# Embedding pieces moved later in the w_out stage, their results kept in the ring of raw pieces, embedding loads and gatings moved, and the last five output blocks started on preset PSUM banks

## The chip, the cores and the metric

The kernel runs on one core of a Trainium2 chip. The metric is device time of one execution in microseconds (us). Several executions are timed; another one is taken by the hardware profiler. Data is float32 throughout. "Piece" below is a block of weights of 128 x 1024 float32 (512 KB): two k-slices of 128 x 512.

## What is computed

One layer: a sliding-window attention mixer, then a per-layer embedding that is added through a gate, then a last norm (512 rows of x, D = 2048).

```python
def reference(x, p, norm_g, final_g, rel_bias, swa_w_in, swa_w_out, ..., ple_proj, ple_norm, ple_gate):
    for i in range(DEPTH):                       # DEPTH = 1, mixer 0
        hn = rmsnorm(x, norm_g[i])
        y = swa_mixer(hn, swa_w_in[j], swa_w_out[j], swa_sinks[j], rel_bias)
...
        x = x + y
        emb = p[i] @ ple_proj[i]                 # 512 x 256 @ 256 x 2048
        g = jax.nn.sigmoid(rmsnorm(x, ple_norm[i]) @ ple_gate[i])
        x = x + emb * g
    return rmsnorm(x, final_g)

def swa_mixer(h, w_in, w_out, sinks, rel_bias):
    q, k, v, gate = jnp.split(h @ w_in, ...)
...
    return (out * jax.nn.silu(gate)) @ w_out
```

## The kernel before

**Precision.** Every product of two float32 matrices is made of three matmuls: each operand is split into a high part (float32r) and the remainder. `mm3` issues the three (lines 126 to 128). For each piece of weights, ScalarE (ACT) casts the raw piece to its high part (`bhi`, line 755) and VectorE (DVE) subtracts for the low part (`blo`, line 756).

**Stages.** First the projections to q, k, v and gate with the attention, then the w_out product, then the ple_gate product, then the last norm and the stores. The w_out and the ple_gate product use a scheme of block products in the manner of Strassen: the products p go in the order 1, 7, 6, 5, 3, 4, each in two column halves jj, each half in four pieces m. "Piece (6,1,2)" is p = 6, jj = 1, m = 2. One piece is 12 matmuls of 512 columns. A further quadrant of each product is computed by the same scheme one level deeper, its "small" products threaded between the pieces (`SMALL`; `small_steps` and `ple_steps` say behind which piece their operands are prepared).

**Embedding.** p @ ple_proj needs nothing of x, so it is threaded into the w_out stage. Nine extra pieces of ple_proj (slots k = 0 to 8), each of 12 matmuls too, stand behind the pieces of w_out that `EMBED_AT` lists. Their accumulators (`eX`, `eO`, `eY`, `eW`, `eZ`) are PSUM banks of 512 columns which are opened by ACT: a slot may begin with a bank that holds minus another one (lines 1253 and 1275), and its matmuls add to it. A finished quadrant (c, jj) is copied by ACT or DVE out of PSUM into an SBUF tile, and GpSimd (POOL) stores it to DRAM (`embeds`, line 1236, 512 KB). Before, there are two such SBUF tiles, `to[0]` and `to[1]`, the two halves of the buffer s2 (in the profile `s`); `to[1]` holds p itself at first. `embed_steps` says behind which pieces p is loaded, split (`make_forms`, DVE lines 1209 to 1221), and the pieces of ple_proj are loaded and summed (`sums0`, `sums1`, DVE lines 1173 and 1174). In the ple_gate stage SP loads the quadrants again into two buffers `e` (`load_embeds`, line 1366, at the places in `embed_loads`), and `gated` applies sigmoid (ACT, line 1379), multiplies by e (DVE, line 1381), adds to x (line 1385, or a POOL DMA that accumulates) and sums squares (line 1396).

**Order.** Each engine runs its instructions in the order of the program. PE and SP have the order of the code throughout; DVE, ACT and POOL have it from the second block product of the ple_gate stage on, before that a scheduler orders them. Raw pieces are requested by SP a fixed number of pieces ahead (`ahead`, line 774: 6 in the "far" range from w_out piece (6,0,0) to the start of the ple_gate stage, 4 after it), and split two pieces ahead of their use. In the far range they lie in a ring of eight buffers of 4 KB a partition, tag `grown`. In the ple_gate stage this ring holds the eight pieces of the last product p = 4.

**End.** The last product p = 4 has weights that are split early (`split_last`, lines 763 and 764, behind the pieces that `early` lists; before: six in p = 3, two behind it). It is computed as blocks (jj, tb) of 24 matmuls: (0,0), (1,0), (0,1), and (1,1) in two parts of 288 and 224 columns. Three of them go to a fresh bank, and DVE subtracts s2 from the result (line 1553); the two parts of (1,1) go to banks that ACT has opened with minus s2 (line 1535). After a block, gate, x and squares follow; finished rows are scaled by 1/norm and final_g (`row`, DVE, line 1414; `by_gain`, DVE, line 1406) and stored.

Of the kernel before, what the change touches and what calls it, by code (L numbers as in the profile page):

```python
# [11 lines left out]
F32 = mybir.dt.float32  # L12
# [6 lines left out]
D = 2048  # L19
# [36 lines left out]
def trunk_kernel(ctx: ExitStack, tc: tile.TileContext, a: dict):  # L56
# [602 lines left out]
    def blk(t):  # L659
# [60 lines left out]
    class Pieces:  # L720
# [48 lines left out]
        def ahead(self, i):  # L769

            last = len(self.specs) - 9
            for n in range(max(i, 0), min(i + 6, last) + 1):
                kind = self.specs[n][0]
                if n not in self.base and n >= self.done and kind not in ("grow", "emb") and (kind == "seed" or n <= i + (6 if far_from <= n < far_to else 4 if i >= far_to else 3)):
# [20 lines left out]
    def add_stage(nm, order):  # L795
# [26 lines left out]
    EMBEDS = {  # L822
        (6, 1): [(1, 0)], (5, 0): [(1, 1), (5, 0)], (5, 1): [(5, 1)], (3, 0): [(3, 0)], (3, 1): [(3, 1)],
    }
# [232 lines left out]
    class Small:  # L1057
# [67 lines left out]
    small_steps = {  # L1125
        (5, 0, 2): 1, (5, 1, 0): 7, (5, 1, 2): 7, (5, 1, 3): 6, (3, 0, 1): 6, (3, 0, 2): 2, (3, 1, 0): 5, (3, 1, 2): 5,
        (3, 1, 3): 4, (4, 0, 1): 3, (4, 0, 3): 3,
    }
# [5 lines left out]
    class Embedding:  # L1134


        def __init__(self, at):
            self.at, self.done = at, 0
            flat = lambda v: v.rearrange("p a b c -> p (a b c)")
            v1, v7 = flat(s1), flat(s7)  # L1140
            self.b1, self.b4, self.b5 = v7[:, :512], v7[:, 512:WE], v7[:, WE:]
            self.b2, self.b3 = v1[:, :WE], v1[:, WE:]
            self.to = [s2[:, n] for n in range(2)]
            self.forms, self.X, self.temp = {}, {}, {}
            self.next = 0
# [7 lines left out]
        def prepare(self, step):  # L1153
# [7 lines left out]
            if step == "p":  # L1161
                load(self.to[1], a["pT"])
            elif step == "forms":
# [28 lines left out]
        def make_forms(self):  # L1192
            r = self.to[1]
            high, low = (late.tile([P, WE], F32R, tag="e", name=f"p_{v}", bufs=2) for v in ("high", "low"))
# [37 lines left out]

        def keep(self, c, jj, n, fill):
            for tb in range(2):
                fill(self.to[n][:, tb], tb)
            nc.gpsimd.dma_start(embeds[c, jj], self.to[n])

        def slot(self):

            k = self.done  # L1240
            jj = 0 if k < 5 else 1
            piece = B.get(self.at[k])
            if k == 0:
                self.left()
            if k in (4, 8):
                self.times(4, piece, 0, self.Z)
                self.keep(4, jj if k == 8 else 0, 1, lambda to, tb: nc.scalar.copy(to, self.Z[tb]))
            if k in (0, 4):
                self.X = self.bank_pair("eX", "t")
                self.times(1, piece, 1 if k else 0, self.X, True)  # L1250
                self.O = self.bank_pair("eO", "o")
                for tb in range(2):
                    nc.scalar.mul(self.O[tb], self.X[tb], -1.0)
            elif k in (1, 5):
                self.times(2, piece, 0, self.O)
                self.times(6, piece, 1, self.X)
                self.keep(1, jj, 0, lambda to, tb: nc.scalar.copy(to, self.O[tb]))
                self.Y = self.bank_pair("eY", "o")
                for tb in range(2):
                    nc.scalar.copy(self.Y[tb], self.X[tb])  # L1260
            elif k in (2, 6):
                self.times(7, piece, 0, self.Y)
                self.times(3, piece, 1, self.X)
                for tb in range(2):
                    nc.scalar.copy(self.left_of[:, tb], self.Y[tb])
                for tb in range(2):
                    nc.scalar.copy(self.to[0][:, tb], self.X[tb])
            elif k in (3, 7):
                self.W = self.bank_pair("eW", "o")
                self.times(5, piece, 0, self.W, True)  # L1270
                self.keep(5, jj, 1, lambda to, tb: nc.vector.tensor_add(to, self.W[tb], self.left_of[:, tb]))
                self.keep(3, jj, 0, lambda to, tb: nc.vector.tensor_add(to, self.W[tb], to))
# [91 lines left out]
    def load_embeds(c, jj):  # L1364
        t = embed_of[c, jj] = late.tile([P, 2, 512], F32, tag="e", name=f"e{c}_{jj}", bufs=2)
        nc.sync.dma_start(t, embeds[c, jj])

    embed_loads = {
        (6, 1, 0): (1, 0), (6, 1, 2): (1, 1), (5, 0, 3): (5, 0), (5, 1, 3): (5, 1), (3, 0, 1): (3, 0), (3, 1, 1): (3, 1),
        (3, 1, 3): (4, 0),  # L1370
# [79 lines left out]
    rooms4 = {}  # L1450
    early = {(3, 0, 0): 0, (3, 0, 2): 1, (3, 1, 0): 2, (3, 1, 1): 3, (3, 1, 2): 4, (3, 1, 3): 5}

# [18 lines left out]
    for n, p in enumerate(ORDER_PLE[:-1]):  # L1471
# [8 lines left out]
        for jj in range(2):  # L1480
            calls = iter(range(4))

            def todo():
# [16 lines left out]
                if k is not None:  # L1500
                    split_last(k)

            def between(m, ps):
# [5 lines left out]
                for q in SMALL["ple_gate"].get((p, jj), {}).get(m, ()):  # L1509
                    small_ple.product(q)  # L1510

            ps = unit(p, jj, at_ple, ple_forms, todo, between)
# [3 lines left out]
            for of, which in EMBEDS.get((p, jj), ()):  # L1516
                e = {t: embed_of[of, which][:, t % 2] for t in ((2, 3) if of == 5 else (0, 1))}
                held_e.update(e)
                if of == 1:
                    later.insert(which ^ 1, partial_of(gate_later, "sum", which, None, dict(e)))  # L1520
                    held_e.clear()
# [9 lines left out]

    def opened_bank(jj, tb, tag, c):

        ps = bank(f"open{jj}_{tb}_{c.start}", tag)
        nc.scalar.mul(ps[:, c], s2[:, jj, tb, c], -1.0)
        return ps

    def block(jj, tb, tag, c=slice(0, 512), share=1.0, opened_ps=None):

        ps = bank(f"last{jj}_{tb}_{c.start}", tag) if opened_ps is None else opened_ps  # L1540
        for k in range(8):
# [3 lines left out]
                ps[:, c], fh[:, k % 2, blk(tb)], fl[:, k % 2, blk(tb)], bh[k % 2][:, c], bl[k % 2][:, c],  # L1545
                k == 0 and opened_ps is None, k == 7, opened_ps is not None,
            )
        e, z = embed_of[4, jj][:, tb], s2[:, jj, tb, c]

        def opened():  # L1550
            if opened_ps is not None:
                return gated(2 + tb, jj, ps[:, c], z, e, c, share)
            nc.vector.tensor_sub(z, ps[:, c], z)
            return gated(2 + tb, jj, z, z, e, c, share)

        return opened

# [6 lines left out]
    load_embeds(4, 1)  # L1564
    split_last(6)
    split_last(7)
    for g in two:
        run(g)
# [5 lines left out]
    next(root)  # L1574
    g = block(0, 0, "s")()
    run(root)
    for step in moved.pop():
        step()
    next(g)
    for j in range(4):  # L1580
        row(0, j, yn2[:, 0:1])
        store(0, j)
    next(g)
    run(g)
    lower, upper = slice(0, 288), slice(288, 512)
    lower_ps = opened_bank(1, 1, "p", lower)
    for j in range(4):
        row(1, j, yn2[:, 1:2])
        store(1, j)
    g = block(1, 0, "s")()  # L1590
    next(g)
# [8 lines left out]
    next(root)  # L1600
    g = block(0, 1, "p")()
    run(root)
    next(g)
    upper_ps = opened_bank(1, 1, "s", upper)
    for j in range(2):
# [8 lines left out]
    base, yn = (const.tile([P, 1], F32, name=f"{v}_3") for v in ("base", "yn"))  # L1614
    g = block(1, 1, "p", lower, opened_ps=lower_ps)()
    next(g)
# [3 lines left out]
    n = done[3]  # L1620
    last = block(1, 1, "s", upper, 1.0 / D, upper_ps)()
    next(last)
# [79 lines left out]
```

## Time and profile before

| | |
|---|---|
| time, median of 3 runs | 807.44 us (807.13, 807.44, 810.07) |
| profiled execution, its own time | 812.43 us |
| its span, first to last instruction | 810.7 us |
| mean granted TensorE clock | 0.986 of full |
| instructions | 11171 |
| ACT busy | 521.4 us |
| DMA, moved | 205.94 MB, mean 254 GB/s |

The durations quoted below come from the profiled execution. A row of the timeline has the start and the duration in us, the engine, the line, the operation, output and inputs by the program's names, shapes, a count of merged instructions, and in brackets how long the engine stood idle before it and what ended this. Matmuls are pipelined: one of 512 columns is listed with 0.39 us at full clock, but the next one starts 0.227 us after it. A row of a window has its bounds, its length, and for each engine the busy us with the count of instructions, then the granted clock, the share of the DMA engines and GB/s.

### The profile page before, as it was taken

How to read it: one execution, taken by the hardware profiler on the slowest of the kernel's cores; microseconds unless marked ns; L12 is line 12 of the kernel's file. 1: busy time of each engine (PE TensorE's matmuls, PEld its weight loads, DVE VectorE, ACT ScalarE, POOL GpSimd, SP SyncE). 2: the span in 40 equal slices, each digit the busy share in tenths (PEclk: the TensorE clock that was granted, in tenths of full speed). 3: DMA queues.
4: the chain of work that ended last, by engine and by line, in shares of the span. 5: the costliest groups of instructions: out<-in, count | busy, mean ns of one | idle time of the engine just before them, and what ended most of it. 6: DMA issues, size and time to landing. Idle time of an engine off the chain costs nothing. (4 is left out here: it accounts for less than half of the span.)

```text
span 810.7 us, 11171 instructions
## 1 busy us (share of the span) xinstructions
PE 786.5 (97%) x3708; PEld 654.8 (81%) x3708; DVE 615.6 (76%) x1057; ACT 521.4 (64%) x1096; POOL 146.8 (18%) x270
## 2 busy tenths in 40 slices
PE   9999999999999999999999998979999999998993
PEld 8888888888888888888888887868888888886783
DVE  4547697868877697768787998747987769978796
ACT  5742676656766576666666555657668966646853
POOL 0201323231323132231311100010000002202100
PEclk9999999999999999999999999989999999999997
DMA  8988999999999999999986698676884499997934
GB/s 332 289 205 285 218 271 299 281 306 248 283 267 282 240 268 275 270 286 249 304 217 176 232 344 293 208 269 207 263 295 173 147 341 272 267 271 196 271 125 135
DMA packets 49961, 205.94 MB, mean 254 GB/s; under 512 B 7456, under 2 KB 8480, under 8 KB 44144
## 3 DMA queue, kind: packets, MB, share of 16 engines
q1 hardware_dynamic: 39152, 154.58, 54.5%
q0 software_dynamic: 10752, 50.66, 30.9%
q8 instruction: 29, 0.48, 0.2%
q14 instruction: 28, 0.23, 0.1%
HBM read 192.31 MB, written 75.55 MB: 330 GB/s over the span
## 5 line engine op out<-in xcount | busy, mean ns | idle before, releaser
L756 DVE TENSOR_TENSOR blo<-braw,bhi 128x1024 fp32r<-128x1024 f32 x100 | 121.4, 1220 | 42.4 <-ACT bhi L755 41.8
L755 ACT CAST bhi<-braw 128x1024 fp32r<-128x1024 f32 x100 | 104.4, 1050 | 41.8 <-PE o L128 16.3
L126 PE MATMUL gps<-xh,whi 128*128 128x512 f32 x256 | 100.0, 390 | 0.0
L127 PE MATMUL gps<-xl,whi 128*128 128x512 f32 x256 | 99.9, 390 | 0.0
L128 PE MATMUL gps<-xh,wlo 128*128 128x512 f32 x256 | 99.7, 390 | 0.0
L126 PE MATMUL qps<-xh,whi 128*128 128x512 f32 x224 | 87.8, 392 | 0.0
L127 PE MATMUL qps<-xl,whi 128*128 128x512 f32 x224 | 87.4, 390 | 0.0
L128 PE MATMUL qps<-xh,wlo 128*128 128x512 f32 x224 | 87.3, 390 | 0.0
L570 POOL TENSOR_SCALAR_AFFINE_SELECT own<-r 64x512 fp32r<-64x512 f32 (+1 forms) x48 | 32.4, 675 | 243.4 <-DVE r L560 243.4
L126 PE MATMUL o<-bhi,fho 128*128 128x512 f32 x192 | 74.9, 390 | 1.4 <-ACT bhi L755 1.4
L127 PE MATMUL o<-blo,fho 128*128 128x512 f32 x192 | 75.1, 391 | 1.2 <-DVE blo L756 1.2
L110 DVE TENSOR_TENSOR wlo<-wraw,whi 128x1024 fp32r<-128x1024 f32 x60 | 73.5, 1226 | 3.0 <-ACT whi L109 2.9
L128 PE MATMUL o<-bhi,flo 128*128 128x512 f32 x192 | 74.8, 389 | 0.0
L556 ACT CAST r<-pt 128x256 fp32r<-128x256 f32 x64 | 23.9, 374 | 69.0 <-PE pt L551 68.8
L126 PE MATMUL g<-bhi,fhg 128*128 128x512 f32 x160 | 63.3, 396 | 2.5 <-DVE s L1430 2.5
L109 ACT CAST whi<-wraw 128x1024 fp32r<-128x1024 f32 x60 | 62.3, 1040 | 4.8 <-issue 4.1
L127 PE MATMUL g<-blo,fhg 128*128 128x512 f32 x160 | 63.5, 397 | 1.7 <-DVE blo L756 1.6
L128 PE MATMUL g<-bhi,flg 128*128 128x512 f32 x160 | 63.1, 394 | 0.0
L128 PEld LDWEIGHTS gps<-xh,wlo 128*128 128x128 f32 x256 | 48.1, 188 | 10.3
L126 PEld LDWEIGHTS gps<-xh,whi 128*128 128x128 f32 x256 | 48.1, 188 | 9.2
L529 ACT ACTIVATE t<-t,sm 128x129 f32<-128x129 f32 (+1 forms) x128 | 49.6, 389 | 8.7 <-DVE sm L525 7.3
L127 PEld LDWEIGHTS gps<-xl,whi 128*128 128x128 f32 x256 | 48.1, 188 | 8.8
(296 smaller groups left out, 1820.4 us busy)
## 6 DMA issues: line engine op xcount, KB each, us to landing
wraw<-in_w_gate_in SPq DMA_DIRECT2D x32, 512.0 KB, 7.9
w_out<-in_w_out POOLq DMA_DIRECT2D x32, 512.0 KB, 9.2
braw<-w_out SPq DMA_DIRECT2D x32, 512.0 KB, 6.0
wraw<-in_w_q SPq DMA_DIRECT2D x28, 512.0 KB, 6.8
braw<-in_w_out SPq DMA_DIRECT2D x22, 512.0 KB, 4.6
braw<-in_ple_gate SPq DMA_DIRECT2D x22, 512.0 KB, 8.1
xw<-in_first SPq DMA_DIRECT2D x14, 640.5 KB, 7.0
w_out<-in_w_out SPq DMA_DIRECT2D x16, 512.0 KB, 11.3
```

Source lines behind the costliest of these rows:

```text
L109: nc.scalar.copy(hi, raw)
L110: nc.vector.tensor_sub(lo, raw, hi.bitcast(F32))
L126: nc.tensor.matmul(ps, sh, mh, start=first, stop=False, skip_group_check=more)
L127: nc.tensor.matmul(ps, sh, ml, start=False, stop=False, skip_group_check=more)
L128: nc.tensor.matmul(ps, sl, mh, start=False, stop=last, skip_group_check=more)
L529: nc.scalar.activation(su, su, AF.Exp, bias=sm[:, u : u + 1], accum_out=sm[:, 2 + u : 3 + u])
L556: nc.scalar.copy(rh, src)
L570: nc.gpsimd.affine_select(out=flat(own), in_=flat(r).bitcast(F32), pattern=[[0, 8], [sign, HB]], compare_op=ALU.is_ge, fill=0.0, base=-HB ...
L755: nc.scalar.copy(hi[:, :n], raw)
L756: nc.vector.tensor_sub(lo[:, :n], raw, hi[:, :n].bitcast(F32))
```

## The change

It has five parts.

1. *Embedding later.* All nine slots stand later, the first behind piece (6,1,0) instead of (6,0,1), the last behind (3,0,0) instead of (5,1,1); the loading of p and the preparation of its operands follow. The small products of the w_out stage start later too and end closer together.
2. *Stores through the ring.* A finished quadrant is kept in a tile of its own out of the ring of eight (`made`) instead of `to[0]` and `to[1]`. p stays in s2. In return raw pieces in the far range are requested 5 ahead instead of 6.
3. *Loads and gatings.* In the ple_gate stage the embeds of three of the quadrants are loaded one to three pieces earlier, and the gating of the quadrants that need no further product (`"sum"`) is queued earlier.
4. *Opened banks.* All last five blocks go to banks that ACT has opened with minus s2 while p = 3 still runs; the three subtractions of line 1553 are gone, and the sigmoid reads PSUM. Seven pieces of the last product are split in p = 3 instead of six.
5. *Rows.* In the end phase of rows 0 to 255, DVE scales column groups 2 and 3, and ACT groups 0 and 1, whose gain DVE has multiplied in during p = 3 (`gains`).

```diff
     SMALL = {
         "w_out": {
-            (5, 1): {2: [1], 3: [1]}, (3, 0): {0: [7], 1: [7], 3: [6]}, (3, 1): {0: [6], 1: [2], 3: [2]},
-            (4, 0): {0: [5], 1: [5], 2: [4], 3: [4]}, (4, 1): {0: [3], 1: [3]},
+            (3, 0): {1: [1], 2: [1], 3: [7]}, (3, 1): {0: [7], 1: [6], 2: [6], 3: [2]},
+            (4, 0): {0: [2], 1: [5], 2: [5], 3: [4]}, (4, 1): {0: [4, 3], 1: [3]},
...
-                if n not in self.base ... n <= i + (6 if far_from <= n < far_to else 4 if i >= far_to else 3)):
+                if n not in self.base ... n <= i + (5 if far_from <= n < far_to else 4 if i >= far_to else 3)):
...
     EMBED_AT = [
-        (6, 0, 1), (6, 0, 2), (6, 1, 0), (6, 1, 1), (6, 1, 3), (5, 0, 0), (5, 0, 2), (5, 0, 3), (5, 1, 1),
+        (6, 1, 0), (6, 1, 1), (6, 1, 3), (5, 0, 0), (5, 0, 2), (5, 0, 3), (5, 1, 1), (5, 1, 2), (3, 0, 0),
...
+        def room(self, c):
+            return late.tile([P, 2, 512], F32, tag="grown", name=f"made{c}_{self.done}", bufs=8)
+
-        def keep(self, c, jj, n, fill):
+        def keep(self, c, jj, fill, to=None):
+            to = self.room(c) if to is None else to
             for tb in range(2):
-                fill(self.to[n][:, tb], tb)
-            nc.gpsimd.dma_start(embeds[c, jj], self.to[n])
+                fill(to[:, tb], tb)
+            nc.gpsimd.dma_start(embeds[c, jj], to)
...
     embed_steps = {
-        (1, 1, 2): "p", (7, 0, 1): "forms", (7, 0, 3): "load0", (7, 1, 1): "sums0", (6, 0, 2): "load1", (6, 0, 3): "load2",
-        (6, 1, 0): "load3", (6, 1, 2): "sums1",
+        (7, 1, 2): "p", (6, 0, 0): "load0", (6, 0, 1): "forms", (6, 0, 2): "sums0", (6, 1, 1): "load1", (6, 1, 2): "load2",
+        (5, 0, 0): "load3", (5, 0, 1): "sums1",
...
     embed_loads = {
-        (6, 1, 0): (1, 0), (6, 1, 2): (1, 1), (5, 0, 3): (5, 0), (5, 1, 3): (5, 1), (3, 0, 1): (3, 0), (3, 1, 1): (3, 1),
+        (6, 0, 3): (1, 0), (6, 1, 1): (1, 1), (5, 0, 1): (5, 0), (5, 1, 1): (5, 1), (3, 0, 1): (3, 0), (3, 1, 1): (3, 1),
...
+    def rows_out(t):
+        for j in (2, 3):
+            row(t, j, yn2[:, t : t + 1])
+            store(t, j)
+        for j in range(2):
+            nc.scalar.mul(x1[j][:, t, :], x1[j][:, t, :], yn2[:, t : t + 1])
+            store(t, j)
...
+    opens = {
+        (3, 1, 0): (0, 0, "t"), (3, 1, 1): (1, 0, "t"), (3, 1, 2): (0, 1, "o"), (3, 1, 3): (1, 1, "o", lower),
+    }
+    gains = {(3, 0, 1): (0, 0), (3, 0, 2): (1, 0), (3, 1, 0): (0, 1), (3, 1, 2): (1, 1)}
...
-            nc.vector.tensor_sub(z, ps[:, c], z)
-            return gated(2 + tb, jj, z, z, e, c, share)
...
+        return gated(2 + tb, jj, ps[:, c], s2[:, jj, tb, c], embed_of[4, jj][:, tb], c, share)
```

On ACT, around slot k = 4 of the embedding (line 1247 before is line 1251 now; `eZ`, `eX`, `eO` are the slot's banks, `s_5037` is s2). Before:

```order
L755 CAST bhi_5659<-braw_5569 128x1024 [waits DMAHW2_49,PE_49,Activation_49]
L865 CAST fho_10_5878<-gate_2333 128x512 [waits PE_49]
L755 CAST bhi_5677<-s_5036 128x1024 [waits DMAHW0_49,PE_49,Activation_49]
L1247 COPY s_5037<-eZ_0_5632 128x512 [waits DMASW2_49,PE_49]
L1247 COPY s_5037<-eZ_1_5633 128x512 [waits PE_49]
L1253 ACTIVATE eO_0_5698<-eX_0_5690 128x512 [waits PE_49,Activation_49]
L1253 ACTIVATE eO_1_5699<-eX_1_5691 128x512 [waits PE_49,Activation_49]
```

and of the change:

```order
L1251 COPY made_4_5753<-eZ_0_5689 128x512 [waits PE_49]
L755 CAST bhi_5743<-s_5036 128x1024 [waits DMAHW2_49,DVE_49,Activation_49]
L1251 COPY made_4_5753<-eZ_1_5690 128x512 [waits PE_49]
L1257 ACTIVATE eO_0_5765<-eX_0_5757 128x512 [waits PE_49,Activation_49]
L1257 ACTIVATE eO_1_5766<-eX_1_5758 128x512 [waits PE_49,Activation_49]
```

The copy waited for a POOL DMA (DMASW, a store of `embeds`) and for PE; now it waits for PE alone.

On SP, in the ple_gate stage around the load of the embeds of quadrant (5,0), tile `e_0`. Before:

```order
L747 DMA braw_7398<-ple_gate_1_2_832 128x1024 [waits DMAHW4_49,DMASW0_49,DVE_49]
L747 DMA braw_7422<-ple_gate_1_3_833 128x1024 [waits DMAHW5_49,DMASW1_49,DVE_49]
L1366 DMA e_0_7445<-embeds_0_5041 128x1024 [waits DMASW2_49,DVE_49]
L747 DMA braw_7448<-in_ple_gate 128x1024 [waits DMAHW6_49,DMAHW3_49,Activation_49]
L747 DMA braw_7471<-in_ple_gate 128x1024 [waits DMAHW7_49,Activation_49]
```

and of the change:

```order
L747 DMA braw_7389<-ple_gate_1_1_831 128x1024 [waits DMAHW3_49,DVE_49]
L1371 DMA e_0_7408<-embeds_0_5041 128x1024
L747 DMA braw_7414<-ple_gate_1_2_832 128x1024 [waits DMAHW4_49,DMAHW1_49,DVE_49]
L747 DMA braw_7438<-ple_gate_1_3_833 128x1024 [waits DMAHW5_49,DVE_49]
L747 DMA braw_7462<-in_ple_gate 128x1024 [waits DMAHW6_49,DVE_49]
```

The load stands two raw pieces earlier and no longer waits for DVE, that is for the gating that reads the buffer's former contents; those who read it are awaited by an earlier instruction of the queue.

On ACT at the end. `open_1_0` and `open_1_288` are the banks of the two parts of block (1,1); `s_5037` is s2. Before:

```order
L1379 ACTIVATE s_5037<-s_5037,rstd_6595 128x512 [waits DVE_49]
L1396 ACTIVATE s_5037,ssq_5035<-x1s 128x512 [waits DVE_49]
L1379 ACTIVATE s_5037<-s_5037,rstd_6595 128x512 [waits DVE_49]
L1535 ACTIVATE open_1_288_7877<-s_5037 128x224
L1609 ACTIVATE x1s<-x1s,yn_7755 128x512 [waits Pool_49]
L1609 ACTIVATE x1s<-x1s,yn_7755 128x512
```

and of the change, where line 1476 opens a bank and line 1387 is the sigmoid:

```order
L763 CAST last_7756<-grown_6975 128x1024 [waits DMASW4_49]
L1476 ACTIVATE open_1_288_7773<-s_5037 128x224 [waits Activation_49]
L1404 ACTIVATE s_5036,ssq_5035<-x1s 128x512 [waits DVE_49] x2
L1404 ACTIVATE s_5038,ssq_5035<-x1s 128x512 [waits DMASW7_49]
L1404 ACTIVATE s_5038,ssq_5035<-x1s 128x512 [waits DMASW0_49]
L1387 ACTIVATE s_5037<-open_0_0_7689,rstd_6603 128x512 [waits PE_49]
```

The opening of the last bank stood behind two sigmoids that wait for DVE; now it stands ahead of all sigmoids of the last blocks.

More of the change, by code (lines that the diff above doesn't have):

```diff
@@ L1142, in __init__ @@
             self.b2, self.b3 = v1[:, :WE], v1[:, WE:]
-            self.to = [s2[:, n] for n in range(2)]
+            self.p = s2[:, 0]
             self.forms, self.X, self.temp = {}, {}, {}
@@ L1161, in prepare @@
             if step == "p":
-                load(self.to[1], a["pT"])
+                load(self.p, a["pT"])
             elif step == "forms":
@@ L1265, in slot @@
                     nc.scalar.copy(self.left_of[:, tb], self.Y[tb])
+                self.upper = self.room(3)
                 for tb in range(2):
-                    nc.scalar.copy(self.to[0][:, tb], self.X[tb])
+                    nc.scalar.copy(self.upper[:, tb], self.X[tb])
             elif k in (3, 7):
@@ L1450, in trunk_kernel, with open_bank @@
     rooms4 = {}
-    early = {(3, 0, 0): 0, (3, 0, 2): 1, (3, 1, 0): 2, (3, 1, 1): 3, (3, 1, 2): 4, (3, 1, 3): 5}
+    early = {(3, 0, 0): 0, (3, 0, 2): 1, (3, 0, 3): 2, (3, 1, 0): 3, (3, 1, 1): 4, (3, 1, 2): 5, (3, 1, 3): 6}
+    lower, upper = slice(0, 288), slice(288, 512)
+    opened = {}
+    def open_bank(jj, tb, tag, c=slice(0, 512)):
+        ps = opened[jj, tb, c.start] = bank(f"open{jj}_{tb}_{c.start}", tag)
+        nc.scalar.mul(ps[:, c], s2[:, jj, tb, c], -1.0)
+    opens = {
+        (3, 1, 0): (0, 0, "t"), (3, 1, 1): (1, 0, "t"), (3, 1, 2): (0, 1, "o"), (3, 1, 3): (1, 1, "o", lower),
+    }
+    gains = {(3, 0, 1): (0, 0), (3, 0, 2): (1, 0), (3, 1, 0): (0, 1), (3, 1, 2): (1, 1)}
     def split_last(k):
@@ L1501, in todo @@
                     split_last(k)
+                if (p, jj, step) in opens:
+                    open_bank(*opens[p, jj, step])
+                if (p, jj, step) in gains:
+                    by_gain(*gains[p, jj, step])
             def between(m, ps):
@@ L1530, in trunk_kernel, with block @@
     f = ple_forms.made[4]
[L1532 to L1540, printed above, removed]
+    def block(jj, tb, c=slice(0, 512), share=1.0):
+        ps = opened[jj, tb, c.start]
         for k in range(8):
@@ L1574, in trunk_kernel @@
     next(root)
-    g = block(0, 0, "s")()
+    g = block(0, 0)
     run(root)
@@ L1579, in trunk_kernel @@
     next(g)
-    for j in range(4):
-        row(0, j, yn2[:, 0:1])
-        store(0, j)
+    rows_out(0)
     next(g)
     run(g)
[L1585 to L1590, printed above, removed]
+    rows_out(1)
+    g = block(1, 0)
     next(g)
@@ L1620, in trunk_kernel @@
     n = done[3]
-    last = block(1, 1, "s", upper, 1.0 / D, upper_ps)()
+    last = block(1, 1, upper, 1.0 / D)
     next(last)
```

40 lines of the change are left out of this document (19 added, 21 removed).

## The prediction

> **What bounds the kernel now.** I read the busy shares first, then the list of waits by engine, then the timeline around each wait, and windows of 10 us where a wait was spread out.
>
> ```profile
> PE 786.5 (97%) x3708; PEld 654.8 (81%) x3708; DVE 615.6 (76%) x1057; ACT 521.4 (64%) x1096; POOL 146.8 (18%) x270
> ...
> PE eO L126 <- ACT eO L1253: 4.1, 1, 4.1
> PE open L126 <- ACT open L1535: 4.0, 1, 4.0
> PE g L126 <- DVE s L1430: 2.5, 1, 2.5
> PE g L127 <- DVE blo L756: 1.6, 3, 0.8
> PE o L126 <- ACT bhi L755: 1.4, 1, 1.4
> PE o L127 <- DVE blo L756: 1.2, 3, 0.8
> ```
>
> PE is busy for 97%, and the changed program issues the same matmuls in the same number. So the change can win only what PE loses in waits, in matmuls at a lowered clock behind them, and at the end. The waits (us in total, times, longest) name four places; A, B, C and D are their names below.
>
> **A, slot k = 4 of the embedding.**
>
> ```profile
> 527.21 1.41 POOL L1236 DMA_DIRECT2D embeds<-s  x2
> 533.40 0.39 PE L128 MATMUL o<-bhi,flo 128*128 128x512 f32 x1
> 536.23 1.07 ACT L1247 COPY s<-eZ 128x512 f32<-128x512 f32 x2 [6.49 <-DMA embeds<-s]
> 537.19 1.09 ACT L1253 ACTIVATE eO<-eX 128x512 f32<-128x512 f32 x2
> 537.85 0.80 PE L126 MATMUL eO<-bhi,p_high 128*128 128x512 f32 x1 [4.06 <-ACT eO L1253]
> 542.95 0.39 PE L126 MATMUL o<-bhi,fho 128*128 128x512 f32 x1
> ...
> DMA to landing us min/median/max: 2.9/7.0/12.6
> embeds<-s POOLq DMA_DIRECT2D x8, 512.0 KB, 5.7
> ```
>
> ACT wants to copy eZ into s2, but the store that POOL issued at 527.21 still reads it: 6.49 us of idle ACT. The opening of eO stands behind the copy, and PE stands 4.06 us. Behind the wait the slot's 12 matmuls take 542.95 - 537.85 = 5.10 instead of 12 x 0.227 = 2.72 (0.227 = 9.77 us over 43 matmuls in a window below), so 2.38 more. Now the copy fills a tile of its own, and its only wait is for PE. Gain 4.06 + 2.38 = **6.4**; nothing, if ACT is late there for another reason (second rival).
>
> **B, DVE's backlog before the embedding.**
>
> ```profile
> 480.00:490.00 10.00, 9.77 (x43) 7.77 (x43) 10.00 (x15) 4.20 (x5) 0.00 (x0) 1.00 0.97 337
> 490.00:500.00 10.00, 7.81 (x34) 5.93 (x33) 9.37 (x13) 5.23 (x7) 1.74 (x2) 1.00 1.00 330
> 500.00:510.00 10.00, 10.00 (x46) 8.28 (x45) 6.07 (x7) 6.05 (x8) 0.00 (x0) 1.00 0.50 160
> 510.00:520.00 10.00, 10.00 (x45) 8.28 (x45) 5.81 (x9) 7.07 (x12) 1.43 (x2) 1.00 0.62 195
> ...
> L1209 DVE TENSOR_TENSOR p_low<-s,p_high 128x512 fp32r<-128x512 f32 x2 | 1.4, 682 | 0.0
> L1174 DVE TENSOR_TENSOR s<-s,s 128x512 f32<-128x512 f32 x1 | 0.7, 686 | 0.0
> L1213 DVE SCALAR_TENSOR_TENSOR p_rest<-s,p_rest 128x256 fp32r<-128x256 f32 x1 | 0.4, 414 | 0.0
> ```
>
> DVE is full, and PE loses 20 - 9.77 - 7.81 = 2.4 there at full clock. The preparation of p and the first sums are five operations of 512 columns and five of 256: 5 x 0.68 + 5 x 0.41 = 5.5 us of DVE. They move behind (6,0,1) and (6,0,2), into the two following windows, where DVE is busy 6.07 and 5.81 of 10. 5.5 us out of a backlog that costs 2.4 ends it: gain **2.4**; bounds 0 (the 2.4 is a late load, DMA share 1.00) and 2.4.
>
> **C, the turn to p = 3 in the ple_gate stage.**
>
> ```profile
> SPq L1366 <- DVE s L1381: 28.6, 6, 11.2
> ...
> 737.07 3.91 SPq L747 DMA_DIRECT2D braw<-in_ple_gate  x4
> 743.53 1.05 ACT L755 CAST bhi<-braw 128x1024 fp32r<-128x1024 f32 x1 [2.42 <-DMA braw<-in_ple_gate]
> 744.62 1.22 DVE L756 TENSOR_TENSOR blo<-braw,bhi 128x1024 fp32r<-128x1024 f32 x1 [2.78 <-ACT bhi L755]
> 746.36 1.28 DVE L1430 TENSOR_TENSOR s<-g,s 128x512 f32<-128x512 f32 x2
> 747.19 0.49 PE L126 MATMUL g<-bhi,fhg 128*128 128x512 f32 x1 [2.48 <-DVE s L1430]
> 750.88 0.42 PE L126 MATMUL g<-bhi,fhg 128*128 128x512 f32 x1
> ```
>
> A load of embeds waits in SP's queue for DVE's gating to free its buffer, in all six times for 28.6 us. The raw pieces queued behind it are issued together from 737.07, and the first lands for ACT at 743.53 after 2.42 us of idle; DVE's additions that free the bank end late, and PE waits 2.48. The next nine matmuls take 750.88 - 747.19 = 3.69 instead of 9 x 0.227 = 2.04, so 1.65 more. In the change this load stands two raw pieces earlier and waits for nothing, since the gatings that read its buffer are queued earlier: gain 2.48 + 1.65 = **4.1**, bounds 0 and 6.0 (with the 1.6 of line 756's waits and some slow matmuls behind them).
>
> [...]
>
> **D, the end.**
>
> ```profile
> 782.50:802.20 19.70, 15.67 (x80) 13.96 (x78) 18.10 (x36) 6.54 (x14) 1.61 (x3) 0.83 0.49 161
> ...
> 789.40 0.29 PE L126 MATMUL open<-last,fhg 128*128 128x288 f32 x1
> 791.02 1.28 DVE L1406 TENSOR_TENSOR x1s<-x1s,fg 128x512 f32<-128x512 f32 x2
> 792.43 0.30 PE L128 MATMUL open<-last,flg 128*128 128x288 f32 x1
> 795.01 0.68 DVE L1553 TENSOR_TENSOR s<-last,s 128x512 f32<-128x512 f32 x1
> 796.36 0.34 ACT L1535 ACTIVATE open<-s 128x224 f32<-128x224 f32 x1
> 796.63 1.32 ACT L1609 ACTIVATE x1s<-x1s,yn 128x512 f32<-128x512 f32 x2
> 796.75 0.55 PE L126 MATMUL open<-last,fhg 128*128 128x224 f32 x1 [4.03 <-ACT open L1535]
> 801.80 0.41 PE L128 MATMUL open<-last,flg 128*128 128x224 f32 x1
> 802.79 0.39 DVE L1381 TENSOR_TENSOR s<-e,s 128x224 f32<-128x224 f32 x1 [0.70 <-ACT s L1379]
> ```
>
> The opening of the last bank (796.36) stands on ACT behind two sigmoids, which wait for DVE's subtractions (795.01): PE stands 4.03. Its 24 matmuls then start 5.05 / 23 = 0.220 apart; those of 288 columns before it, 3.03 / 23 = 0.132 apart, so at that clock 224 columns take 0.132 x 224 / 288 = 0.102: 24 x (0.220 - 0.102) = 2.8, and I count 2.65 for the gap's uneven first step. So PE could end 6.7 earlier. But DVE is busy 18.10 of 19.70 here, and the end follows from its last chain (802.79 on), not from PE. Of DVE's work in the end phase the change takes three subtractions (3 x 0.64, half of the 1.28 for two), four rows (4 x 0.70, now on ACT) and one split (1.22): 5.9. ACT's 6.54 get four multiplications (4 x 0.66 = 2.6). Putting the changed order's rows of DVE and ACT behind each other with these durations, the gatings of (0,1) still queue behind rows and gains, and the last chain starts 4.3 to 6.7 earlier. I take **4.7**, nearer the engines' chain than PE's.
>
> **What the change adds.** In p = 3, between the splits of its first and last piece, DVE has 10 wide operations (1.22) and 13 narrow ones (0.64) before: 20.5 us, against 7 x 2.72 = 19.0 of PE. Now it has 11 wide ones (one more early split) and 11 narrow ones, gains included, since gatings have moved ahead: 13.42 + 7.04 = 20.5. So DVE is no freer there, and its lead of two pieces is used up as before; ACT gets four openings (4 x 0.66) and a cast (1.05) in a stage where it has idle time. I charge **0.6** for the openings that stand ahead of casts, bounds 0 and 3. The small products, now at most two behind one piece at the end of w_out, the sums that follow their loads by one step less, and the shorter lookahead I charge with **1.0** together; bounds 0 and 3, the latter about one wait of the size of C.
>
> Sum: 6.4 + 2.4 + 4.1 + 4.7 - 0.6 - 1.0 = **16.0**. The profiled execution gives 812.43 - 16.0 = 796.4. The median of the runs is 5.0 below the profiled one. If those 5.0 are a fixed cost of profiling, the time is 807.44 - 16.0 = 791.4; if the plain runs have 5.0 less of these very stalls, 796.4. I lean to the first: **792.5**. The low end has every gain at its bound and no charge: 807.44 - (6.4 + 2.4 + 6.0 + 6.7) = 786.
>
> **Rivals.**
>
> First, *DVE becomes the bound of p = 3 and of the end*. For it: 20.5 us of DVE against 19.0 of PE, and four gains and a split that now stand between the splits. Then C returns as a wait for `blo` with its slow matmuls (4.1 lost), and the end gains 1.5 instead of 4.7: 16.0 - 7.3 = 8.7, or 807.44 - 8.7 = 799. Against it: the count of DVE work there is the same as before. Chance 0.20.
>
> Second, *the change doesn't do what it says*: ACT reaches the copy of eZ late for another reason (it is busy with casts, or the ring tile isn't free), SP's loads of embeds still hold the raw pieces, and the end is bound by DVE. A and C stay, D gains 1.5: 807.44 - (2.4 + 1.5 - 1.6) = 805. Against it: the copy's only listed wait is PE. Chance 0.05.
>
> Third, slower: *the ring of raw pieces becomes the bound*. The eight `made` tiles take eight turns in the ring of eight, and in SP's order seven raw loads of the far range now wait for a POOL DMA, a store of embeds, to land.
>
> ```profile
> braw<-in_w_out SPq DMA_DIRECT2D x22, 512.0 KB, 4.6
> ```
>
> A raw piece is cast two pieces before its use. Requested five ahead, it has 3 x 2.72 = 8.2 us, needs 4.6 to land, and has 3.6 left. A store takes 7.0 (median above) from its issue. If each of the seven loads is issued as late as the store's landing allows, and the store only when the copy is made at the time the slot ends, each costs 7.0 - 3.6 = 3.4: 24, and 807.44 - 16 + 24 = 815. It decides from the point where a store is issued less than 3.4 us ahead of the load that takes its place. Against it: loads of the ring take turns, so a tile comes back only after seven others. Chance 0.08. [...]
>
> **Chances.** Forecast 0.67, first rival 0.20, second 0.05, third 0.08. The range 786 to 802 holds the forecast's case and the first rival with some room. A change of 0.5% (4 us) is about what a measurement of this kernel can tell: forecast and first rival are faster (0.87), the second is the same (0.05), the third slower (0.08).
>
> **What will show it.** In the changed profile: the list of PE's waits has no eO behind ACT and no `open` behind ACT (A, D); the copy of eZ shows no idle time that ends with a DMA (A); the windows of 10 us ahead of the embedding have PE at 10.00 (B); the loads of embeds wait for DVE for much less than 28.6 (C); in the last window the granted clock is near 1 instead of 0.83, and the last chain starts some 4.7 us sooner after the last block begins. SP's waits of line 747 for a DMA of embeds, or PE waits for `bhi` behind a late raw piece between the slots, speak for the third rival; PE waits for `blo` in p = 3 for the first. I am wrong if a new wait of 3 us or more, with slow matmuls behind it, shows in either stage.

## The result and the profile after

| | before | after |
|---|---|---|
| time, median of 6 runs | 808.63 us (807.13 to 812.01) | 798.56 us (797.14 to 798.90) |
| ratio | | 0.9868 (95% interval 0.9847 to 0.9889) |
| profiled execution, own time | 812.43 us | 798.63 us |
| its span | 810.7 us | 796.9 us |
| mean granted TensorE clock | 0.986 | 0.993 |

The six runs of the kernel before are the three of the table further up and three more. The change is faster by 10.1 us (1.3%), forecast were 14.9 (807.44 - 792.5). In the profiled executions it is 13.8, forecast were 16.0.

PE's row of the busy shares and PE's longest waits in the changed kernel (us in total, times, longest):

```profile
PE 781.4 (98%) x3708; PEld 650.7 (82%) x3708; DVE 613.9 (77%) x1054; ACT 525.6 (66%) x1103; POOL 147.0 (18%) x270
...
PE g L126 <- ACT bhi L755: 2.6, 1, 2.6
PE g L127 <- DVE blo L756: 2.1, 3, 0.8
```

The waits of A (eO) and of D (`open`) are gone, so are those for `o` (B). What stands first now is a wait for a cast, in the place of C.

The windows of the changed kernel at the places of B and A, and the copy of eZ that had waited 6.49 us for a store:

```profile
480.00:490.00 10.00, 10.00 (x46) 8.29 (x45) 8.89 (x11) 5.18 (x7) 0.00 (x0) 1.00 0.97 354
490.00:500.00 10.00, 10.00 (x45) 8.27 (x45) 8.88 (x13) 5.49 (x9) 0.00 (x0) 1.00 1.00 364
530.00:540.00 10.00, 10.00 (x46) 8.29 (x45) 7.53 (x9) 7.58 (x13) 2.85 (x4) 1.00 0.95 268
...
559.38 1.05 ACT L1251 COPY made<-eZ 128x512 f32<-128x512 f32 x2
```

PE is full at full clock in all three (9.77, 7.81 and 5.94 before), and the copy has no bracket: ACT came to it without idle time.

To see where the rest went, I compare the start of three instructions that both kernels have: POOL's twelfth accumulating load of line 734, the first matmul of 288 columns near the end, and the end of the span. Rows of POOL's timeline from there on, before:

```profile
701.96 0.87 POOL L734 DMA_DIRECT2D grown<-in_ple_gate  x1 [3.02 <-DVE blo L756]
705.99 0.86 POOL L734 DMA_DIRECT2D grown<-in_ple_gate  x1 [3.17 <-DVE blo L756]
710.60 0.88 POOL L734 DMA_DIRECT2D grown<-in_ple_gate  x1 [3.74 <-DVE blo L756]
714.66 0.87 POOL L734 DMA_DIRECT2D grown<-in_ple_gate  x1 [3.18 <-DVE blo L756]
736.57 1.76 POOL L1383 DMA_DIRECT2D x1s<-s  x2 [21.04 <-PE g L128]
737.72 1.51 POOL L734 DMA_DIRECT2D grown<-in_ple_gate  x1
```

and after, with the cast on ACT, the matmuls of PE behind it, two windows, and PE's and DVE's rows of the end:

```profile
690.93 0.87 POOL L734 DMA_DIRECT2D grown<-in_ple_gate  x1 [3.01 <-DVE blo L756]
710.79 1.79 POOL L1391 DMA_DIRECT2D x1s<-s  x2 [18.99 <-DVE s L1389]
711.94 3.34 POOL L734 DMA_DIRECT2D grown<-in_ple_gate  x3
723.36 1.77 POOL L1391 DMA_DIRECT2D x1s<-s  x2 [8.08 <-DVE s L1389]
724.51 1.52 POOL L734 DMA_DIRECT2D grown<-in_ple_gate  x1
...
742.99 1.04 ACT L755 CAST bhi<-braw 128x1024 fp32r<-128x1024 f32 x1 [5.10 <-DMA braw<-in_ple_gate]
744.08 0.70 PE L126 MATMUL g<-bhi,fhg 128*128 128x512 f32 x1 [2.62 <-ACT bhi L755]
751.05 0.39 PE L128 MATMUL g<-bhi,flg 128*128 128x512 f32 x1
...
700.00:710.00 10.00, 10.00 (x46) 8.29 (x45) 8.51 (x10) 6.49 (x8) 0.00 (x0) 1.00 0.49 170
720.00:740.00 20.00, 18.45 (x77) 13.90 (x77) 12.77 (x15) 9.88 (x18) 4.43 (x5) 1.00 1.06 283
...
781.15 0.29 PE L126 MATMUL open<-last,fhg 128*128 128x288 f32 x1
786.86 0.27 PE L128 MATMUL open<-last,flg 128*128 128x224 f32 x1
788.99 0.38 DVE L1389 TENSOR_TENSOR s<-e,s 128x224 f32<-128x224 f32 x1
```

| stretch | before | after | forecast |
|---|---|---|---|
| start to the twelfth load | 701.96 | 690.93: 11.0 less | A + B - 1.0: 7.8 less |
| to the first matmul of 288 columns | 87.44 | 90.22: 2.8 **more** | C - 0.6: 3.5 less |
| to the end | 21.3 | 15.75: 5.6 less | D: 4.7 less |

The middle stretch went the wrong way. The rows say how: before, the loads of line 734 go out every 4 us up to the fifteenth, and only the sixteenth and last stands behind two adds of a gated quadrant to x (line 1383, 1391 after) and goes out at 737.72. After, the gating of quadrant "sum 0" is queued earlier, so two of its adds stand ahead of four of these loads in POOL's order, and two more ahead of the last. The first two wait 18.99 us for DVE's multiplication, and the loads stay behind them. Three loads that were due at some 695, 700 and 704 (11.0 ahead of their times before) go out together at 711.94. The DMA engines are busy for half of the time from 700 to 710 (0.49) and all of it from 720 to 740 (1.06). In this burst a raw piece comes late: ACT stands 5.10 us, PE 2.62, and then PE runs at half pace (matmuls start 0.43 us apart from 745.93 to 751.05, instead of 0.227; the granted clock is 0.50 from 744.22 to 751.04). That the order on POOL is the cause was an inference then; the experiments test it.

### The profile page after: what moved, and what is told of

It reads as the page before. It is cut to its first block, busy times and chain, and to the rows that moved or that the text cites. A ratio compares the mean times of both kernels' runs of the same rounds, so it can differ in the third digit from the quotient of the medians.

```text
span 796.9 us, 11160 instructions
## 1 busy us (share of the span) xinstructions
PE 781.4 (98%) x3708; PEld 650.7 (82%) x3708; DVE 613.9 (77%) x1054; ACT 525.6 (66%) x1103; POOL 147.0 (18%) x270
## 5 line engine op out<-in xcount | busy, mean ns | idle before, releaser
L560 DVE TENSOR_TENSOR r<-pt,r 128x256 fp32r<-128x256 f32 x56 | 23.7, 424 | 41.0 <-ACT r L556 40.3
```

The costliest lines, as they stand in the source:

```text
L560: nc.vector.tensor_sub(rl, src, rh.bitcast(F32))
```

## The experiments

All were run beside the kernel before, in four batches; a ratio is to the kernel before of the same batch. "Loss" is PE's: the time between starts of matmuls above 0.227 us each, summed over a stretch of the profiled execution. Times of runs of one batch I compare to about 1 us; this is an estimate from the changed kernel, whose medians in two batches are 798.56 and 798.34.

**Which part brings what: parts alone**

Parts 1 and 2 on the kernel before (the embedding's places, the ring):

```diff
-        (6, 0, 1), (6, 0, 2), (6, 1, 0), ... (5, 1, 1),
+        (6, 1, 0), (6, 1, 1), (6, 1, 3), ... (3, 0, 0),
...
+            to = self.room(c) if to is None else to
```

> The kernel before with parts 1 and 2 of the change alone (embedding later, stores through the ring, lookahead 5). If A and B are as predicted and the profiled 812.43 of before is a normal execution: 6.4 + 2.4 less, 798 to 801 us, with the waits for eO behind ACT and for bhi near 490 gone. If part of A is only in the profiled execution (the plain runs of before are 3.8 shorter than it): 802 to 803. If the ring binds (third rival): 805 or more, and PE waits for bhi between the slots. The turn to p = 3 and the end stay as before.

Measured: 800.60 us, ratio 0.988 (0.9855 to 0.9905). The first case; no wait between 430 and 590, so the ring binds nothing.

Part 2 alone, and part 1 alone:

```diff
-            nc.gpsimd.dma_start(embeds[c, jj], self.to[n])
+            nc.gpsimd.dma_start(embeds[c, jj], to)
```

> The kernel before with part 2 alone (stores through the ring, lookahead 5), the embedding at its old places. If A is the copy's wait for the store of its old tile, as predicted: eO's wait of 4 us is gone, B, C and D stay, 6.4 less in the profile, 801 to 804 us, and the runs agree within 2 us if A is also what makes the kernel before scatter. If A has another reason (second rival): the wait stays, 808 to 810.

```diff
     EMBED_AT = [
-        (6, 0, 1), (6, 0, 2), (6, 1, 0), ...
+        (6, 1, 0), (6, 1, 1), (6, 1, 3), ...
```

> The kernel before with part 1 alone (embedding and its preparation later), still stored from the two tiles of s2, lookahead 6. As predicted, B's 2.4 goes since DVE's backlog near 490 is gone, and A stays in some slot, at 3 to 7 us: 804 to 808 us, with the runs scattered over 5 us or more as before. If the shift alone also ends A: 799 to 802.

Measured: 802.34 (0.991, 0.9888 to 0.9932) with part 2 alone, 803.90 (0.9921, 0.9899 to 0.9944) with part 1 alone; the kernel before ran at 809.67 beside them. The list of PE's waits with part 2 alone, then with part 1 alone, with the row of eO's matmul:

```profile
PE open L126 <- ACT open L1540: 3.9, 1, 3.9
PE g L127 <- DVE blo L756: 3.3, 4, 1.0
PE g L126 <- ACT bhi L755: 1.5, 1, 1.5
PE o L127 <- DVE blo L756: 1.2, 2, 1.0
```

```profile
PE open L126 <- ACT open L1535: 3.9, 1, 3.9
PE g L127 <- DVE blo L756: 2.3, 3, 0.8
PE g L126 <- DVE s L1430: 2.1, 1, 2.1
PE eO L126 <- ACT eO L1253: 1.0, 1, 1.0
...
539.05 0.50 PE L126 MATMUL eO<-bhi,p_high 128*128 128x512 f32 x1 [1.01 <-ACT eO L1253]
```

The ring alone ends eO's wait, and B's wait for `bhi` too; `o` still waits 1.2 for `blo`. The shift alone ends the waits for `o`, and cuts eO's wait from 4.06 to 1.01. So both parts ease A, and their gains, 7.3 and 5.8, add up to more than the 9.6 of the two together. I had expected the shift to leave A at 3 us or more, at 804 to 808 us and with the runs scattered over 5; they lie within 2.2 (802.86 to 805.03). With part 2 alone the time is as expected, but its runs lie within 3.0 (801.95 to 804.91), not within 2.

Parts 4 and 5 on the kernel before:

```diff
+    opens = {
+        (3, 1, 0): (0, 0, "t"), (3, 1, 1): (1, 0, "t"), ...
...
-            nc.vector.tensor_sub(z, ps[:, c], z)
```

> The kernel before with parts 4 and 5 alone (opened banks, one more early split, gains in p = 3, rows on ACT). PE theory of the end, as the traces read: 6.75 gained by PE, 1.15 given back behind its last matmul, so 5.6 less: 803 us. If gains and the early split cost time in p = 3 (first rival): the waits for blo between 750 and 770 grow and the time is 805 or more. A and B stay.

Measured: 804.99 (801.63 to 809.04), ratio 0.9938 (0.9918 to 0.9959). 5.2 us less than the 810.20 beside it, against 5.6 expected; A and B stay (eO waits 4.0). The waits of PE's `g` for `blo` grow from 1.6 to 3.3 us, which is the sign of the first rival, and the time is at that rival's border of 805; PE's wait for DVE's additions out of its bank falls from 2.5 to 0.7.

**Part 3: does it cost, and is it the order on POOL?**

The changed kernel with part 3 undone:

```diff
-        (6, 0, 3): (1, 0), (6, 1, 1): (1, 1), (5, 0, 1): (5, 0), (5, 1, 1): (5, 1), ...
+        (6, 1, 0): (1, 0), (6, 1, 2): (1, 1), (5, 0, 3): (5, 0), (5, 1, 3): (5, 1), ...
...
-                if (p, jj, m) == (6, 1, 1):
-                    later.append(partial_of(gate_later, "sum", 0, None, embeds_for(1, 0)))
```

> The changed kernel with part 3 undone (loads of embeds and gatings at their places of before). POOL theory (the gating of sum 0 stands ahead of four accumulating loads in POOL's queue and holds three of them for 8 to 17 us, so they fall into one burst): the loads are spread again, PE loses in the turn to p = 3 some 7 us as before instead of 10, 795 to 796.5 us. DVE theory (the gains and splits of p = 3 make the stall): no difference, 798 to 799. Prediction's theory (the earlier loads of embeds free 4): slower by 4, 802.

Measured: 795.81 (795.05 to 796.33), ratio 0.9818 (0.9794 to 0.9843): 2.5 to 2.8 us faster than the changed kernel, which ran in two other batches, and none of its runs there (797.14 to 798.95) is as fast. Part 3 as it stands costs time; my forecast of 4 us for it is refuted. On POOL the thirteenth to fifteenth loads go out at 695.37, 699.98 and 704.05 again; the sixteenth still stands behind two adds and goes out at 724.92.

The adds of the sum quadrants behind the last accumulating load, first version:

```diff
+        if t < 2 and j < 2:
+            held_adds.append(partial_of(nc.gpsimd.dma_start, xt, z, accum_op=ALU.add))
...
+                if not B.due:
+                    while held_adds:
+                        held_adds.pop(0)()
```

> The changed kernel, but the accumulating stores to x of the sum quadrants are issued on POOL only when the last accumulating load of weights (line 734) has been issued; everything else stays. POOL theory: the three held loads go out one by one near 695, 700 and 704, DMA share between 700 and 710 rises above 0.49, the raw pieces land in time, and of the 10 us lost from 720 to 760 at least 5 are gone: 790 to 793 us. Traffic theory (the earlier loads of embeds fill the DMA engines wherever the adds stand): no change, 797 to 799. DVE theory: the same, with waits for blo.

Measured: 794.55 (793.81 to 795.15), ratio 0.9803 (0.9778 to 0.9828). In this version squares on ACT fall behind the multiplication of x by the gain (line 1418, first at 743.97). They square other values, so it does not compute the layer; the instructions are the same ones, and only its time is of use. PE's loss from 720 to 760 falls from 10 to 5.2. It is 1.5 us above the expected 793, and since squares were displaced too, it doesn't settle the matter. So the squares were put right behind the adds, and the changed kernel itself was run beside it:

```diff
+                    while moved:
+                        later.extend(moved.pop(0))
```

> The changed kernel unaltered, as the measure for the three runs beside it: 797 to 799.5 us, ratio 0.985 to 0.989, with the wait of PE behind a late raw piece near 744 again.

> As the run with the adds behind the accumulating loads, with the squares of the sum quadrants queued right behind the adds, so that they come ahead of the gates of p = 3. POOL theory: the loss between 720 and 760 is 5 us or less instead of 10, 790 to 795 us. If the gain of that run came only from its displaced squares: 797 to 799.

Measured: the changed kernel 798.34 (797.71 to 798.95), ratio 0.9855 (0.9826 to 0.9884); this one 796.09 (794.81 to 797.00), ratio 0.9825 (0.9795 to 0.9855), a loss of 8.0 instead of 5 or less. The waits of ACT between 720 and 760, and PE's longest, show a new place:

```profile
ACT s L1408 <- DMA x1s<-s: 5.3, 3, 2.8
...
PE g L126 <- ACT bhi L755: 3.2, 1, 3.2
```

The squares, queued too early now, wait for the adds to land, and the casts stand behind them. So the squares had to stay where the changed kernel has them:

```diff
+                    for _ in range(len(held_adds) // 2):
+                        later.extend(moved.pop(0))
```

> The changed kernel with the adds of the sum quadrants behind the last accumulating load on POOL, and the squares on ACT exactly where the changed kernel has them. POOL theory: no burst from 711, no squares that wait for late adds; the loss between 720 and 760 is 5 us or less, 791 to 795 us. Traffic theory: the raw pieces of p = 3 still land after 11 us and PE waits 2 us or more for a cast near 744: 796 to 799.

Measured: **790.00 us** (789.67 to 791.01), ratio 0.9765 (0.9737 to 0.9794), a little better than expected. SP and PE have the order of the changed kernel, ACT and DVE too but for one sigmoid and one multiplication that come two or three places later; POOL has the adds behind the loads. Rows of POOL, the list of PE's waits but for the first warm-up, and the first matmul of 288 columns of this kernel:

```profile
690.87 0.87 POOL L734 DMA_DIRECT2D grown<-in_ple_gate  x1 [3.01 <-DVE blo L756]
694.90 0.87 POOL L734 DMA_DIRECT2D grown<-in_ple_gate  x1 [3.17 <-DVE blo L756]
699.51 0.88 POOL L734 DMA_DIRECT2D grown<-in_ple_gate  x1 [3.74 <-DVE blo L756]
703.58 0.88 POOL L734 DMA_DIRECT2D grown<-in_ple_gate  x1 [3.18 <-DVE blo L756]
705.91 0.87 POOL L734 DMA_DIRECT2D grown<-in_ple_gate  x1 [1.46 <-DVE blo L756]
710.73 1.76 POOL L1524 DMA_DIRECT2D x1s<-s  x2 [3.96 <-DVE s L1391]
...
PE g L127 <- DVE blo L756: 0.6, 1, 0.6
...
772.31 0.29 PE L126 MATMUL open<-last,fhg 128*128 128x288 f32 x1
```

The loads go out at 694.90, 699.51 and 703.58, where they were due, and one wait of 0.6 is left of C. The middle stretch takes 772.31 - 690.87 = 81.4, 6.0 less than before. It is not the amount of traffic: between 700 and 750 more is moved here than in the changed kernel (14.30 against 12.74 MB), but spread out. The median time of the raw pieces from issue to landing in that stretch, in the changed kernel and here:

```profile
braw<-in_ple_gate SPq DMA_DIRECT2D x8, 512.0 KB, 11.6
braw<-ple_gate SPq DMA_DIRECT2D x6, 512.0 KB, 4.6
```

```profile
braw<-in_ple_gate SPq DMA_DIRECT2D x8, 512.0 KB, 5.7
braw<-ple_gate SPq DMA_DIRECT2D x6, 512.0 KB, 9.2
```

The pieces that PE had waited for (`in_ple_gate`) land in half the time. The six others (`ple_gate`), which are now under way together with the loads of POOL, take twice as long, and PE does not wait for them.

A different edit with the same aim, the accumulating loads requested three pieces earlier:

```diff
-                self.due.append((i + (2 if self.specs[i][0] == "seed" else 6), n))
+                self.due.append((i + (2 if self.specs[i][0] == "seed" else 3), n))
```

> The changed kernel with the accumulating loads of the last product requested three pieces behind the use of their tile instead of six, so that two of the four that stood behind the adds of sum 0 now stand ahead of them. POOL theory: two of the three loads leave the burst of 711; part of the gain of the run beside it, 794 to 797.5 us. If the order on POOL is not the cause: 797.5 to 799.

Measured: 792.38 (792.09 to 793.14), ratio 0.9794 (0.9763 to 0.9826), better than expected. Two loads still stand behind the adds and go out at 711.87; two of four in the burst are enough to bring back a loss of 3.6 between 720 and 760, against 1.3 in the run beside it.

**The charges**

Part 5 undone, on the kernel with the squares behind the adds:

```diff
-    gains = {(3, 0, 1): (0, 0), (3, 0, 2): (1, 0), (3, 1, 0): (0, 1), (3, 1, 2): (1, 1)}
+    gains = {}
...
+        for j in range(4):
+            row(t, j, yn2[:, t : t + 1])
```

> The run before it with part 5 undone as well (four rows of each block on DVE, no gains in p = 3). If the gains delay the splits of p = 3 (first rival, my charge of 0.6): the waits for blo between 740 and 760 shrink by 1 to 2 us, but DVE's end has four rows more of 0.70 less four gains: 2.8 us more on its chain, of which some is covered; 0 to 2 us slower altogether. If gains cost nothing in p = 3: 2 to 3 us slower.

Measured: 796.86 (796.38 to 797.06), ratio 0.9836 (0.9804 to 0.9868), 0.8 slower than its partner. The last matmul of this kernel, then of the partner:

```profile
783.19 0.27 PE L128 MATMUL open<-last,flg 128*128 128x224 f32 x1
```

```profile
785.22 0.27 PE L128 MATMUL open<-last,flg 128*128 128x224 f32 x1
```

Without the gains PE is done 2.0 us earlier, but both spans are 795.3 us: behind the last matmul DVE, with four rows more, gives it back. So part 5 is worth about 1 us at most, and the intervals of the two ratios overlap.

Lookahead 6 again:

```diff
-(5 if far_from <= n < far_to
+(6 if far_from <= n < far_to
```

> The changed kernel with raw pieces of the far range requested 6 ahead again. The charge for the shorter lookahead: if the ring of eight has room for 6 beside the made tiles, no difference from the changed kernel (within 1 us), which says that the shorter lookahead cost nothing. If the ring is tight (third rival), the loads wait for the stores of embeds and PE waits for bhi between 540 and 600: 2 us slower or more.

Measured: 798.29 (797.01 to 798.73), ratio 0.9852 (0.9823 to 0.9882), the same as the changed kernel beside it. The shorter lookahead costs nothing that shows.

## Why the prediction was right, and where it was wrong

**A and B held.** The waits went as written, and runs of the parts alone show that the ring alone removes eO's wait. The stretch gained 11.0, 3.2 more than the 7.8 of the sum. Counted by starts of matmuls, B was 0.8 larger than I took it for: the two windows of the prediction hold 43 + 34 = 77 matmuls, those of the changed kernel 46 + 45 = 91, and 14 x 0.227 = 3.2 us, not 2.4. My 2.4 came from the busy time, which lists the matmul behind a wait as longer (0.50 instead of 0.39) and so hides a part of the loss. A was 0.2 larger in the same way: 537.85 - 533.40 - 0.227 + 2.38 = 6.6. Another 0.8 is not the change's: the first matmul of line 126 starts at 6.87 in the profile before and at 6.03 in the one after, long before anything that the change moves. And the charge of 1.0 did not show (lookahead: no difference; PE has no wait between 430 and 690). That is 2.8 of the 3.2.

**C failed, in one sentence of it**: "gain 2.48 + 1.65 = 4.1", on the ground that the load of embeds stands earlier and waits for nothing. That step looked at SP's queue and at DVE's count and not at POOL's. A gating issues four kinds of instruction, one of them a DMA of POOL that adds to x. Moving the gating moved two such adds ahead of four loads where before two stood ahead of one, and they wait for DVE. The rows show it: the two adds go out at 710.79 after 18.99 us of waiting, and three of the loads right behind them at 711.94. The place of a few adds in POOL's queue was worth 0.9855 against 0.9765, or 798.3 against 790.0 us, each beside its own kernel before. What I wrote of SP held for the load it named: the load of (5,0) goes out at 712.75, right behind the raw piece ahead of it, and the next four raw pieces go out between 713.74 and 722.56 instead of within 3.91 us. All loads of embeds together still wait 21.1 us for DVE, instead of 28.6. With the adds behind the loads, the stretch gains 6.0, which is the upper bound I gave to C. But this does not show that the freed load is worth 4.1 or more: in that run the sixteenth load, which stood behind adds before the change too, has been freed as well (705.91), and no run has the adds behind the loads with part 3 undone.

**D held**: 5.6 against 4.7 within 4.3 to 6.7. From the first matmul of 288 columns to its last matmul PE takes 5.71 instead of 12.40 (789.40 to 801.80), 6.7 less as computed; behind the last matmul the end takes 10.0 instead of 8.9, so 1.1 is given back to DVE's chain. I had put this at 2.0.

**The charge for p = 3** (0.6) has not been checked by itself. With POOL's order mended, one wait of 0.6 is left, but this agreement is luck: the waits for `blo` grew by 1.7 with parts 4 and 5 alone, and PE was done 2.0 earlier without the gains. The first rival (DVE as the bound) did not come about: what binds in the changed kernel is a raw piece that lands late (ACT's row at 742.99), and its waits for `blo`, 2.1 us, are 0.6 in the run with the adds behind the loads. That the measured 798.56 is the number of this rival (799) is chance, and the range holds it because it was drawn to hold this rival; the forecast itself, 792.5, is 6.1 off. The sign that I had named for being wrong, a new wait of 3 us or more with slow matmuls behind it, is nearly there: 2.62 us, and 0.56 one matmul later.

**The third rival** is half there. SP's waits of line 747 in the changed kernel between 500 and 620, and the landing time of stores from the ring:

```profile
SPq L747 <- DMA embeds<-made: 24.3, 5, 6.2
...
DMA to landing us min/median/max: 2.9/3.6/8.0
```

Raw loads do wait for stores, five times and for 24.3 us in all. (That I had feared 24 us is chance: those were PE's.) But PE does not wait for any of these pieces. The prediction also read its price wrongly: its 7.0 us is the median over all transfers that touch `embeds`, the later loads of `e` included. The row for the stores alone, shown beside it, says 5.7; at that price the same sum gives 7 x (5.7 - 3.6) = 15 instead of 24, that is 806 instead of 815. Now a store takes 3.6. Why stores landed later before was not tried.

**From the profile to the median.** I took the 5.0 us between the profiled execution and the median for mostly fixed. It is not: the profiled execution of the changed kernel is 0.1 from its median. The kernel before scatters, from 806.35 to 812.97 in eleven runs beside the control, and its profiled execution was one of the long ones. With both parts of the embedding in, four runs lie within 1.6 us (800.12 to 801.72); with the end alone changed, twelve lie within 7.4. So the scatter seems to go with A and B, and part of the 11.0 gained there is not in the medians. Of the 4.9 us by which the gain was over-forecast, 2.2 are in the sum (11.0 instead of 7.8, a loss of 2.8 instead of a gain of 3.5, 5.6 instead of 4.7), and 2.7 are this step. The 2.2 are small only by luck: the first and the last stretch gained 4.1 more than their terms, which covers most of the 6.3 by which the middle one fell short.

## What to carry to other kernels

When a piece of work is moved, list what each of its instructions issues on every queue, and what then stands behind it there: here a DMA that waited 18.99 us for DVE held back the loads behind it in the same queue. Held transfers came out as a burst (three at 711.94), and what was late then was another queue's load, some 30 us further on (the cast that waited 5.10 us for it starts at 742.99). Before a profiled execution is used as the base of a sum, compare it with the spread of plain runs: here it was one of the long ones (812.43 against a median of 807.44), and of the 13.8 us gained against it the medians had 10.1.

## What the runs showed that was not expected

In these runs the length of a wait does not decide by itself whether slow matmuls follow. These are the same two matmuls, with the same waits in front of them, and what follows: first in the kernel before, then in the run of parts 4 and 5 alone, whose program is the same up to there:

```profile
494.40 0.50 PE L126 MATMUL o<-bhi,fho 128*128 128x512 f32 x1 [1.43 <-ACT bhi L755]
495.66 0.51 PE L127 MATMUL o<-blo,fho 128*128 128x512 f32 x1 [0.76 <-DVE blo L756]
496.01 0.39 PE L128 MATMUL o<-bhi,flo 128*128 128x512 f32 x1
```

```profile
493.57 0.50 PE L126 MATMUL o<-bhi,fho 128*128 128x512 f32 x1 [1.43 <-ACT bhi L755]
494.83 0.51 PE L127 MATMUL o<-blo,fho 128*128 128x512 f32 x1 [0.76 <-DVE blo L756]
495.67 0.63 PE L127 MATMUL o<-blo,fho 128*128 128x512 f32 x1
496.10 0.63 PE L128 MATMUL o<-bhi,flo 128*128 128x512 f32 x1
```

In the first, matmuls go on at 0.227 us; in the second, they start 0.43 us apart from 495.67 to 498.66. The steps on either side (0.28 us from 495.39, 0.38 us from 498.66) put the bounds of the half pace at 495.56 and 498.98, as an estimate. A single wait of 2.09 us, with part 1 alone, left slow matmuls too (0.43 us apart from 739.30 to 742.29); one of 1.56 with one of 0.47 shortly before it, in the first version with late adds, left none (0.34 us, then 0.24 apart). So 2.19 us of idle time in two parts were followed by slow matmuls once, and by none another time.

What these profiles do show is slow stretches that fit one step. In the kernel before the granted clock is 0.50 from 535.89 to 542.71 and from 747.51 to 750.93: 6.82 and 3.42 us, twice and once 3.41, and the two starts are 211.62 us apart, 62 x 3.413. In the changed kernel the stretch from 744.22 to 751.04 is twice 3.41 again. In the run of parts 4 and 5 alone the two starts, 495.56 and by the same kind of estimate 539.95, are 44.39 apart, 13 x 3.415. So where a wait falls between two such steps may be what decides; no run here tests this.

And a wait that is cut from 4.06 to 1.01 loses its slow matmuls too (behind it they start 0.34 us, then 0.23 apart), which is one reason why the two parts of the embedding's change were worth more apart than together.
